# Products of ones on TensorE ahead of long waits, column sums 64 wide, and a two-part split by VectorE alone

## The chip, the cores and the metric

The kernel runs on one core of one Trainium2 chip. The metric is the device time of one execution in microseconds, as the median of several runs. A profiled execution has a time of its own; its span runs from the first to the last instruction that the profile shows.

## What is computed

Three blocks of a transformer follow each other on one sequence of 512 tokens with 1024 features, all in float32. The first mixes an mLSTM (a gated recurrence written as attention with decays) with differential attention, and adds a feed-forward part and a gated side input. The second has four layers; those that matter here are a stick-breaking attention and one with latent queries and keys. The third has a gated feed-forward part, a mixer of spatial gating and forgetting attention, and another feed-forward part. Each part begins with a norm over the features, and this is what the change is about.

```python
def rmsnorm(x, g):
    xf = x.astype(jnp.float32)
    y = xf * lax.rsqrt(jnp.mean(xf * xf, -1, keepdims=True) + EPS)
    return (y * g.astype(jnp.float32)).astype(x.dtype)
...
def first_block(x, p, ...):
    h = rmsnorm(x, norm_mix_g[l])
    proj = h @ w_in[l]
    mq, mk, mv, mo, mi, mf, dq, dk, dv, gates = jnp.split(proj, split_idx, axis=-1)
    ...
    hm = mlstm_chunkwise(heads(mq_c, M_HEADS), heads(mk_c, M_HEADS), heads(mv, M_HEADS), i_pre, f_pre)
    ya = (jax.nn.sigmoid(mo) * hm) @ w_br_m[l]
    ...
    x = x + mixed @ w_out[l]
    h = rmsnorm(x, norm_ffn_g[l])
    u = causal_dwconv(h @ w_up[l], ffn_conv_w[l], ffn_conv_b[l])
    x = x + (jax.nn.gelu(gt) * val) @ w_down[l]
    hg = rmsnorm(x, norm_ple_g[l])
    x = x + jax.nn.sigmoid(hg @ w_ple_gate[l]) * (p[l].astype(x.dtype) @ w_ple[l])
    return rmsnorm(x, norm_final_g)
...
def reference(x, p, ...):
    x = first_block(x, p, ...)
    x = second_block(x, ...)
    return third_block(x, c_3, ...)
```

## The kernel before

**Tiles.** Activations lie with features on the 128 partitions and the 512 tokens along the free axis, as eight tiles of 128x512. A weight matrix is read in pieces of 128x1024 by DMA into `raw`. For precision each operand is split into two parts of a shorter float type, a high part and the rest: `hi` and `lo` for activations (`split`), `wh` and `wl` for weights (`load`). ScalarE (ACT) rounds the high part, VectorE (DVE) subtracts it for the rest. A matmul into a PSUM tile `pm` is then three products, hi x wh, lo x wh, hi x wl (`mm`, L429 to L431; `mm_tok`, L439 to L441, with tokens as the output's rows and 256 columns).

**A norm.** `Norm.add` squares each tile (ACT) and adds it up in `acc` (DVE). `colsum` then sums over the partitions on TensorE (PE): for each block of 128 tokens one product of `acc` with a column of ones, into one PSUM tile; `add_pe` does the same from each squared tile, where the sums of eight tiles are collected in PSUM. `rstd` goes on with `ms_eps` (DVE, tile `ms`, L577) and `rpow` (GpSimd, tile `rc`, L572, the power of -1/2), and `bcast_ps` (L584, tile `bc`) puts the result on all partitions by four products, or two where a turn treats half of the tokens (`rows`). Everything that is scaled by the norm waits for that. What PE has to do meanwhile is other work that doesn't need the norm: the first products of the next projection, whose rows are scaled later.

**Order.** Each engine takes its instructions in the order in which the program has them. A scheduler sets that order from the code, the priorities and its own table of costs, so that a new instruction also moves others. PSUM is shared out in pools: three tiles for `pm`, one for sums and broadcasts (`ms`), two for scores, one each for two other roles. A reader of a PSUM tile waits for the writes into that tile that stand ahead of it in the program.

**The first stage.** `decays` builds, for each of four blocks of tokens, the row `R` of the recurrence's decay: a running sum on DVE, and `parts`, which clears R (L407), rounds the high part on ACT (L408) and subtracts on DVE (L409). `columns` then transposes the columns `cc` on PE into `cps` (L676) and copies them to `ccol` (DVE, L677). ACT needs `ccol` for the decay matrix `DT` (L834), which starts from `pd` (PE, L831); `num` (L838) is the product with the values `vt` (copied from `pm` by ACT, L816). In the same stretch DVE works through a product for the third block (`adaw`, L1408), one weight tile at a time, as its DMA comes in; SyncE issues it when a `raw` tile is free, which is when a `wl` has been made.

Of the kernel before, what the change touches and what calls it, by code (L numbers as in the profile page):

```python
# [23 lines left out]
EPS = 1e-6  # L24
NEG = -1e30
# [212 lines left out]
class Norm:  # L238
# [21 lines left out]
    def add_pe(self, k, x, sl):  # L260

        net, nc = self.net, self.net.nc
        sq = net.q(F32, "sq")
        nc.scalar.activation(sq[:, sl], x[:, sl], AF.Square)
        if k == 0:
            self.cols = net.psa("colsum")
        for j, o in enumerate(range(sl.start, sl.stop, P)):
            nc.tensor.matmul(self.cols[:, j:j + 1], sq[:, o:o + P], net.ones[:, 0:1], start=k == 0 and j == 0, stop=k == 7, skip_group_check=True)

    def rstd(self, sl=ALL):  # L270
        net = self.net
        n = (sl.stop - sl.start) // P
        ps = net.colsum(self.acc, sl) if self.cols is None else self.cols[:, :n]
        self.cols = None
        return net.rpow(net.ms_eps(ps, self.n, n), n)

    def stats(self):
        rc = self.rstd()
        return self.net.bcast([rc[:, j:j + 1] for j in range(NB)]), rc

    def rows(self, sl, role):

        rc = self.rstd(sl)
        return self.net.bcast_ps([rc[:, j:j + 1] for j in range((sl.stop - sl.start) // P)], role)


class Net:
    def __init__(self, ctx, tc, d):
# [14 lines left out]
        self.dp = pool("dp", 1, space=bass.MemoryType.DRAM)  # L303
        self.vec = self.const([P, NV], F32, "vec")
# [84 lines left out]

    def split(self, src):  # L390
        nc = self.nc
        h, l = self.t(F32R, "hi"), self.t(F32R, "lo")
        nc.scalar.copy(h, src)  # L393
        nc.vector.tensor_tensor(l, src, h.bitcast(F32), ALU.subtract)  # L394
        return h, l
# [8 lines left out]
    def parts(self, out, src, n, sl=ALL):  # L404

        nc = self.nc
        nc.vector.memset(out.bitcast(F32)[:, sl], 0.0)  # L407
        nc.scalar.copy(out[0:n, sl], src[0:n, sl])  # L408
        nc.vector.tensor_tensor(out[64:64 + n, sl], src[0:n, sl], out[0:n, sl].bitcast(F32), ALU.subtract)  # L409
# [144 lines left out]
    def colsum(self, acc, sl=ALL):  # L554

        ps = self.psa("colsum")
        n = (sl.stop - sl.start) // P
        for j in range(n):
            o = sl.start + j * P
            self.nc.tensor.matmul(ps[:, j:j + 1], acc[:, o:o + P], self.ones[:, 0:1], start=True, stop=True)  # L560
        return ps[:, 0:n]
# [18 lines left out]
    def bcast_ps(self, cols, role="ms", ps=None):  # L580

        ps = self.psa("bc", role) if ps is None else ps
        for j, col in enumerate(cols):
            self.nc.tensor.matmul(ps[:, j * P:(j + 1) * P], col.to_broadcast([P, P]), self.ident, start=True, stop=True)  # L584
# [35 lines left out]
    def block1(self, third):  # L620
# [10 lines left out]
        with self.tc.issue_after(self.last.ins):  # L631
            self.constants()
            self.wide = True
            self.lead(first, xg, w, [ALL])
# [37 lines left out]
        def columns():  # L672
            ps = self.psa("cps")
            with self.tc.issue_after(self.pe.ins):
# [277 lines left out]
    def ffn1(self, norm):  # L952
# [3 lines left out]
        rb, _ = norm.stats()  # L956
# [32 lines left out]
    def ple(self, norm):  # L989
# [12 lines left out]
        rb, _ = norm.stats()  # L1002
# [17 lines left out]
    def final_norm(self, na, nb):  # L1020
# [4 lines left out]
        pb = self.colsum(nb.acc)  # L1025
        mb = self.s(NB, "mb")
# [42 lines left out]
    def stick_breaking(self, xg, rb, rc, norm):  # L1069
# [43 lines left out]
        for grp in range(4):  # L1113
# [6 lines left out]
            for c in range(2):  # L1120
                last = self.sb_pair(*cur, c, o[2 * grp + c], pre)
            self.fill_all()
            cur = nxt
        with self.tc.issue_after(last.ins):
# [3 lines left out]
    def sb_pair(self, q, k, vt, c, out, pre):  # L1128
# [15 lines left out]
        for tiles, blocks in (((0, 1, 2), (1, 2, 3)), ((3, 4), (0,))):  # L1144
# [38 lines left out]
            for sb in blocks:  # L1183
                for par in range(2):
                    col = (sb % 2) * 256 + (2 * c + par) * 64
                    nc.tensor.matmul(po[ROWS[par], sb * P:], vt[sb // 2][:, col:col + 64], reg(pr, sb, par), start=sb == 1, stop=sb == 0, skip_group_check=True)
# [3 lines left out]
    def mla(self, norm, third):  # L1190
# [6 lines left out]
        rb, rc = norm.stats()  # L1197
# [130 lines left out]
        for f in (work[0], gates[1], work[1], gates[2], work[2]):  # L1328
            f()
        for c in range(4):  # L1330
# [189 lines left out]
    def hybrid(self, x, first):  # L1520
# [93 lines left out]
        def branch_rstd(norm):  # L1614
            norm.rc = norm.rstd()

        def branch(name, norm, ys, at):

            rb = self.bcast([norm.rc[:, j:j + 1] for j in range(NB)])
            for k in range(4):  # L1620
# [40 lines left out]
        branch_rstd(nb)  # L1661
# [155 lines left out]
```

## Time and profile before

| what | us |
|---|---|
| three runs, median (lowest to highest) | 2471.32 (2469.2 to 2471.55) |
| the profiled execution | 2467.3 |
| its span | 2465.5 |
| PE busy | 2401.9 |
| DVE, ACT, GpSimd busy | 1327.3, 990.7, 67.0 |
| start to start of products into `pm`, full clock: 512 columns | 0.23 |
| the same, 256 columns | 0.12 |

The profile has a page of sums (busy time by engine, costliest groups of instructions, DMA issues) and views of the trace: waits by line, a timeline, and the busy time of an engine in chosen stretches with the clock that TensorE was granted there (1.00 is 2.4 GHz, 0.50 is 1.2 GHz). In a timeline row stand the start, the duration, the engine, the line and operation with output and input, how many were joined in the row, and in brackets how long the engine had been idle and what released it. A product in float32 of 128 columns appears as two passes, so x8 is four products.

### The profile page before, as it was taken

The numbers are of one execution on the slowest core, as the hardware profiler recorded it, in microseconds if no ns is written. First come the engines' busy times: TensorE is split into PE (matmuls) and PEld (weight loads), VectorE is DVE, ScalarE is ACT, GpSimd is POOL, SyncE is SP. The second block draws the span as 40 slices with busy tenths as digits, with TensorE's granted clock in tenths as the row PEclk, the third lists the DMA queues.
The fourth block names the chain that finished last, engine by engine and source line by source line (L and its number), as shares of the span: only waits on it lengthen the run. The fifth ranks groups of instructions, "written<-read, shape, count | busy, mean of one in ns | idle before, by whom it ended". The sixth has DMA issues, their size and how long they took to land. (4 is left out here: it accounts for less than half of the span.)

```text
span 2465.5 us, 30961 instructions
## 1 busy us (share of the span) xinstructions
PE 2401.9 (97%) x12430; PEld 1979.6 (80%) x12430; DVE 1327.3 (54%) x2240; ACT 990.7 (40%) x1579; POOL 67.0 (3%) x66
## 2 busy tenths in 40 slices
PE   8999999999999999999999999999999989999998
PEld 6877778888888787776877798888898768888887
DVE  7536556774775664445666954323364565432333
ACT  5423433442343445665334633232235444322221
POOL 0000000000000000000010000000010002000001
PEclk9999999999999999999999999999999999999999
DMA  5222225433433432222301323232222211223221
GB/s 190 95 91 94 94 97 181 141 127 97 161 125 114 132 109 84 71 78 77 107 29 62 114 84 120 86 107 98 87 68 87 81 43 52 94 88 109 94 94 43
DMA packets 71743, 240.74 MB, mean 98 GB/s; under 512 B 8232, under 2 KB 11184, under 8 KB 71600
## 3 DMA queue, kind: packets, MB, share of 16 engines
q1 hardware_dynamic: 71600, 238.78, 29.2%
q8 instruction: 97, 1.59, 0.3%
q14 instruction: 46, 0.38, 0.1%
HBM read 236.64 MB, written 2.11 MB: 97 GB/s over the span
## 5 line engine op out<-in xcount | busy, mean ns | idle before, releaser
L429 PE MATMUL pm<-hi,wh 128*128 128x512 f32 (+1 forms) x2736 | 1044.2, 383 | 9.4 <-ACT hi L393 5.7
L430 PE MATMUL pm<-lo,wh 128*128 128x512 f32 (+1 forms) x2736 | 1041.6, 381 | 0.4 <-DVE lo L394 0.4
L431 PE MATMUL pm<-hi,wl 128*128 128x512 f32 (+1 forms) x2736 | 1040.6, 381 | 0.0
L419 ACT CAST wh<-raw 128x1024 fp32r<-128x1024 f32 (+1 forms) x372 | 382.0, 1029 | 783.9 <-PE pm L430 536.2
L420 DVE TENSOR_TENSOR wl<-raw,wh 128x1024 fp32r<-128x1024 f32 (+1 forms) x372 | 444.8, 1196 | 441.7 <-ACT wh L419 416.8
L429 PEld LDWEIGHTS pm<-hi,wh 128*128 128x128 f32 x2736 | 517.6, 189 | 108.7 <-issue 7.7
L430 PEld LDWEIGHTS pm<-lo,wh 128*128 128x128 f32 x2736 | 517.2, 189 | 97.9 <-issue 3.5
L431 PEld LDWEIGHTS pm<-hi,wl 128*128 128x128 f32 x2736 | 517.1, 189 | 96.5 <-issue 3.4
L439 PE MATMUL pm<-wh,hi 128*128 128x256 f32 x400 | 116.0, 290 | 6.2 <-ACT vt L816 4.9
L1408 DVE CUSTOM_DVE_ANT_0 adaw<-adaw,cb 128x1024 f32<-128x1024 f32 x72 | 87.9, 1220 | 53.9 <-DMA adaw<-in_w_ada 53.6
L441 PE MATMUL pm<-wh,lo 128*128 128x256 f32 x400 | 114.5, 286 | 0.0
L440 PE MATMUL pm<-wl,hi 128*128 128x256 f32 x400 | 114.0, 285 | 0.0
L572 POOL TENSOR_TENSOR rc<-ms,nhalf 128x4 f32<-128x4 f32 (+3 forms) x33 | 42.2, 1278 | 2301.2 <-DVE ms L577 1865.0
L1487 DVE TENSOR_TENSOR sg<-sg,pm 128x512 f32<-128x512 f32 x44 | 30.2, 687 | 133.3 <-PE pm L431 133.3
L439 PEld LDWEIGHTS pm<-wh,hi 128*128 128x128 f32 x400 | 77.6, 194 | 7.2 <-ACT vt L816 5.3
L440 PEld LDWEIGHTS pm<-wl,hi 128*128 128x128 f32 x400 | 77.6, 194 | 0.4 <-issue 0.2
L441 PEld LDWEIGHTS pm<-wh,lo 128*128 128x128 f32 x400 | 77.6, 194 | 0.2
L481 PE MATMUL pm<-hi,wh 128*128 128x256 f32 (+1 forms) x216 | 61.5, 309 | 10.2 <-ACT hi L400 7.1
L970 DVE SCALAR_TENSOR_TENSOR uy<-ur,vec,uy 128x511 f32<-128x511 f32 x88 | 65.7, 748 | 9.0 <-ACT uy L968 8.0
L258 DVE TENSOR_TENSOR acc<-acc,sq 128x512 f32<-128x512 f32 (+1 forms) x93 | 54.8, 595 | 27.6 <-ACT sq L254 26.4
L482 PE MATMUL pm<-lo,wh 128*128 128x256 f32 (+1 forms) x216 | 66.2, 308 | 0.3 <-DVE lo L1439 0.3
L483 PE MATMUL pm<-hi,wl 128*128 128x256 f32 (+1 forms) x216 | 66.1, 309 | 0.0
(350 smaller groups left out, 2344.5 us busy)
## 6 DMA issues: line engine op xcount, KB each, us to landing
raw<-in_w_gu SPq DMA_DIRECT2D x88, 512.0 KB, 3.2
adaw<-in_w_ada SPq DMA_DIRECT2D x72, 512.0 KB, 3.2
raw<-in_w_dn SPq DMA_DIRECT2D x48, 512.0 KB, 3.2
raw<-in_w_up SPq DMA_DIRECT2D x44, 512.0 KB, 3.3
raw<-in_w_g SPq DMA_DIRECT2D x16, 512.0 KB, 3.3
raw<-in_w_l0qk SPq DMA_DIRECT2D x16, 512.0 KB, 3.3
raw<-in_w_l SPq DMA_DIRECT2D x12, 512.0 KB, 3.2
X<-in_x SPq DMA_DIRECT2D x16, 256.0 KB, 6.6
```

The source lines that it names most:

```text
L419: nc.scalar.copy(wh[:, :n], raw[:, :n])
L420: nc.vector.tensor_tensor(wl[:, :n], raw[:, :n], wh[:, :n].bitcast(F32), ALU.subtract)
L429: self.nc.tensor.matmul(out, a, xh, start=start and k == 0, stop=False)
L430: self.nc.tensor.matmul(out, a, xl, start=False, stop=False)
L431: self.pe = self.nc.tensor.matmul(out, b, xh, start=False, stop=stop and k == n - 1)
L439: self.nc.tensor.matmul(out, xh[:, sl], a, start=start and k == 0, stop=False)
L440: self.nc.tensor.matmul(out, xh[:, sl], b, start=False, stop=False)
L441: self.pe = self.nc.tensor.matmul(out, xl[:, sl], a, start=False, stop=stop and k == len(x) - 1)
L482: self.nc.tensor.matmul(o[:, sl], wh[:, k], xl[:, sl], start=False, stop=False)
L483: self.nc.tensor.matmul(o[:, sl], wl[:, k], xh[:, sl], start=False, stop=k == 7)
L970: nc.vector.scalar_tensor_tensor(y[:, sh:], raw[:, :S - sh], self.v("fconv_w", 44 * (2 - sh) + f), y[:, sh:], mult, add)
L1408: nc.vector.tensor_tensor_reduce(w, w, cb, 0.5, 0.0, ALU.mult, ALU.add, mod[:, i:i + 1])
```

## The change

Four edits. **Sums**: the products that sum over partitions take 64 columns of ones instead of one and write 64 equal columns; the reader takes every 64th. **Products of ones**: a new `busy(n)` issues n products of a 128x128 tile of ones with itself into columns 256 to 383 of a PSUM tile that nothing else uses there. It is called at 17 places, for 212 products in all: 36 before the first projection, 24 ahead of the transposes in `columns`, 6, 16, 8, 9, 10 and 16 after the sums of six norms, 26 at the end of the stick-breaking attention, 22 before the first scores of the latent attention, 15 after the broadcast in the mixer's second branch, and 4 after the sums of the second half in six turns. **Split**: `parts` rounds on DVE instead of ACT (four times in `decays`, once in the mixer). **Constant**: the tile of ones is set at the start by DVE.

```diff
 EPS = 1e-6
+CW = 64
 NEG = -1e30
...
         for j, o in enumerate(range(sl.start, sl.stop, P)):
-            nc.tensor.matmul(self.cols[:, j:j + 1], sq[:, o:o + P], net.ones[:, 0:1], start=k == 0 and j == 0, stop=k == 7, skip_group_check=True)
-    def rstd(self, sl=ALL):
+            net.pe2 = nc.tensor.matmul(self.cols[:, j * CW:(j + 1) * CW], sq[:, o:o + P], net.ones[:, :CW], start=k == 0 and j == 0, stop=k == 7, skip_group_check=True)
+    def rstd(self, sl=ALL, busy=0):
         net = self.net
         n = (sl.stop - sl.start) // P
-        ps = net.colsum(self.acc, sl) if self.cols is None else self.cols[:, :n]
+        if self.cols is None:
+            ps, bank = net.colsum(self.acc, sl), net.sums_bank
+        else:
+            ps, bank = self.cols[:, 0:n * CW:CW], self.cols
         self.cols = None
+        net.busy(busy, [net.pe2], bank)
         return net.rpow(net.ms_eps(ps, self.n, n), n)
-    def stats(self):
-        rc = self.rstd()
+    def stats(self, busy=0):
+        rc = self.rstd(busy=busy)
         return self.net.bcast([rc[:, j:j + 1] for j in range(NB)]), rc
...
-        rc = self.rstd(sl)
+        rc = self.rstd(sl, 4 if sl.start else 0)
         return self.net.bcast_ps([rc[:, j:j + 1] for j in range((sl.stop - sl.start) // P)], role)
...
         self.dp = pool("dp", 1, space=bass.MemoryType.DRAM)
+        self.one_sq = self.const([P, P], F32, "one_sq")
+        nc.vector.memset(self.one_sq, 1.0)
         self.vec = self.const([P, NV], F32, "vec")
...
+    def busy(self, n, after=(), bank=None):
+        if n == 0:
+            return
+        bank = self.psa("busy", "tr") if bank is None else bank
+        with ExitStack() as ctx:
+            for i in after:
+                ctx.enter_context(self.tc.issue_after(i.ins))
+            for _ in range(n):
+                self.nc.tensor.matmul(bank[:, 256:256 + P], self.one_sq, self.one_sq, start=True, stop=True, skip_group_check=True)
...
         nc.vector.memset(out.bitcast(F32)[:, sl], 0.0)
-        nc.scalar.copy(out[0:n, sl], src[0:n, sl])
+        nc.vector.tensor_copy(out[0:n, sl], src[0:n, sl])
         nc.vector.tensor_tensor(out[64:64 + n, sl], src[0:n, sl], out[0:n, sl].bitcast(F32), ALU.subtract)
...
-        ps = self.psa("colsum")
+        ps = self.sums_bank = self.psa("colsum")
         n = (sl.stop - sl.start) // P
...
             o = sl.start + j * P
-            self.nc.tensor.matmul(ps[:, j:j + 1], acc[:, o:o + P], self.ones[:, 0:1], start=True, stop=True)
-        return ps[:, 0:n]
+            self.pe2 = self.nc.tensor.matmul(ps[:, j * CW:(j + 1) * CW], acc[:, o:o + P], self.ones[:, :CW], start=True, stop=True)
+        return ps[:, 0:n * CW:CW]
...
         for j, col in enumerate(cols):
-            self.nc.tensor.matmul(ps[:, j * P:(j + 1) * P], col.to_broadcast([P, P]), self.ident, start=True, stop=True)
+            self.pe2 = self.nc.tensor.matmul(ps[:, j * P:(j + 1) * P], col.to_broadcast([P, P]), self.ident, start=True, stop=True)
         return ps
...
             self.wide = True
+            self.busy(36, (), self.psa("busy"))
             self.lead(first, xg, w, [ALL])
...
             ps = self.psa("cps")
+            self.busy(24, [self.pe], ps)
             with self.tc.issue_after(self.pe.ins):
...
         xg = norm.x
-        rb, _ = norm.stats()
+        rb, _ = norm.stats(6)
         nxt = Norm(self, lambda k: self.v("norm_ple", k))
...
                 pe.append(e)
-        rb, _ = norm.stats()
+        rb, _ = norm.stats(16)
         gg = self.const([P, 8], F32, "gg")
...
         pb = self.colsum(nb.acc)
+        self.busy(8, [self.pe2], self.sums_bank)
         mb = self.s(NB, "mb")
...
                 last = self.sb_pair(*cur, c, o[2 * grp + c], pre)
+            ends = [self.pe2]
             self.fill_all()
             cur = nxt
+        self.busy(26, [*ends, self.pe])
         with self.tc.issue_after(last.ins):
...
                     col = (sb % 2) * 256 + (2 * c + par) * 64
-                    nc.tensor.matmul(po[ROWS[par], sb * P:], vt[sb // 2][:, col:col + 64], reg(pr, sb, par), start=sb == 1, stop=sb == 0, skip_group_check=True)
+                    self.pe2 = nc.tensor.matmul(po[ROWS[par], sb * P:], vt[sb // 2][:, col:col + 64], reg(pr, sb, par), start=sb == 1, stop=sb == 0, skip_group_check=True)
         nc.vector.tensor_copy(out, po)
...
         nc.sync.dma_start(sin, d["cs_tab"][:, S:2 * S])
-        rb, rc = norm.stats()
+        rb, rc = norm.stats(9)
         lat = {}
...
             f()
+        self.busy(22, [self.pe2, self.pe])
         for c in range(4):
...
-        def branch_rstd(norm):
-            norm.rc = norm.rstd()
+        def branch_rstd(norm, busy=10):
+            norm.rc = norm.rstd(busy=busy)
...
             rb = self.bcast([norm.rc[:, j:j + 1] for j in range(NB)])
+            if at:
+                self.busy(15, [self.pe2])
             for k in range(4):
...
         self.flush()
-        branch_rstd(nb)
+        branch_rstd(nb, 16)
         self.fill_all()
```

The new instructions move others. On DVE in the first stage, behind the last part of R; `wl` belongs to weights that come in, `adaw` to the third block. Before:

```order
L409 TENSOR_TENSOR R<-G,R 4x128
L420 TENSOR_TENSOR wl<-raw,wh 128x1024
L677 COPY ccol<-cps 128x16
L420 TENSOR_TENSOR wl<-raw,wh 128x1024
L837 SCALAR_TENSOR_TENSOR DT<-sT,DT 128x512
L837 SCALAR_TENSOR_TENSOR DT<-sT,DT 128x384
L1408 ISA adaw,mod<-adaw,cb 128x1024
```

and now:

```order
L427 CAST R<-G 4x128
L428 TENSOR_TENSOR R<-G,R 4x128
L439 TENSOR_TENSOR wl<-raw,wh 128x1024 x2
L1433 ISA adaw,mod<-adaw,cb 128x1024
L1433 ISA mod 128x1
L698 COPY ccol<-cps 128x16
L858 SCALAR_TENSOR_TENSOR DT<-sT,DT 128x512
L858 SCALAR_TENSOR_TENSOR DT<-sT,DT 128x384
```

`ccol` stood behind one `wl` and stands now behind two and the step on `adaw`.

On PE at the same place, from the transposes on; before:

```order
L676 MATMUL cps<-cst,cc 128x4 x4
L831 MATMUL pd<-R,pick 128x512
L832 LDWEIGHTS bf_ident
L832 MATMUL pd<-bf_mask_t,bf_ident 128x128
L836 MATMUL sT<-cy 128x512
L439 MATMUL pm<-wh,hi 128x256
L440 MATMUL pm<-wl,hi 128x256
```

and now:

```order
L407 MATMUL cps<-one_sq 128x128 x24
L697 MATMUL cps<-cst,cc 128x4 x4
L852 MATMUL pd<-R,pick 128x512
L853 LDWEIGHTS bf_ident
L853 MATMUL pd<-bf_mask_t,bf_ident 128x128
L857 MATMUL sT<-cy 128x512
L852 MATMUL pd<-R,pick 128x384
```

Eleven products into `pm` that stood between `sT` and the second `pd` have moved behind it.

On PE at the norm at 821 us (the one ahead of the gated side input); before:

```order
L560 MATMUL colsum<-ones,acc 128x1 x4
L429 MATMUL pm<-hi,wh 128x512
L430 MATMUL pm<-lo,wh 128x512
L431 MATMUL pm<-hi,wl 128x512
L429 MATMUL pm<-hi,wh 128x512
L430 MATMUL pm<-lo,wh 128x512
L431 MATMUL pm<-hi,wl 128x512
L429 MATMUL pm<-hi,wh 128x512
L584 MATMUL bc<-cst,rc 128x128 x4
```

and now:

```order
L579 MATMUL colsum<-ones,acc 128x64 x4
L407 MATMUL colsum<-one_sq 128x128 x16
L448 MATMUL pm<-hi,wh 128x512
L449 MATMUL pm<-lo,wh 128x512
L603 MATMUL bc<-cst,rc 128x128 x4
L450 MATMUL pm<-hi,wl 128x512
```

The sixteen products stand between the sums and `bc`, in the tile of the sums, and five of seven products into `pm` have moved behind `bc`.

## Rows read from the trace of the kernel before

**Rows 1.** the page's first part: engine, busy us (share of the span), instructions
```profile
PE 2401.9 (97%) x12430; PEld 1979.6 (80%) x12430; DVE 1327.3 (54%) x2240; ACT 990.7 (40%) x1579; POOL 67.0 (3%) x66
```

**Rows 2.** PE's waits: waiter, releaser, us in total, times, longest us
```profile
PE bc L584 <- POOL rc L572: 14.0, 17, 2.3
PE pm L481 <- ACT hi L400: 7.1, 1, 7.1
PE pm L429 <- ACT hi L393: 5.7, 2, 3.4
...
PE mls L1340 <- ACT p L1349: 4.6, 3, 2.8
...
PE pm L439 <- ACT p L1349: 1.3, 1, 1.3
```

**Rows 3.** half-clock stretches: us, PE busy (instructions), granted clock, DMA share, GB/s
```profile
85.15:91.98 6.83, 4.63 (x21) 0.50 0.19 72
825.84:829.25 3.41, 3.41 (x12) 0.50 0.42 139
1163.76:1167.17 3.41, 3.12 (x7) 0.50 0.00 0
1214.96:1218.37 3.41, 3.41 (x12) 0.50 0.02 5
1293.47:1296.88 3.41, 3.41 (x16) 0.50 0.00 0
1839.60:1843.01 3.41, 3.41 (x15) 0.50 0.78 279
2006.85:2013.68 6.83, 5.92 (x18) 0.50 0.00 0
2030.75:2037.57 6.82, 4.69 (x11) 0.50 0.06 26
2088.77:2095.60 6.83, 6.58 (x32) 0.50 0.23 79
```

**Rows 4.** PE's timeline, 128x128 passes: start us, us, operation, xcount
```profile
1268.36 1.95 PE L584 MATMUL bc<-cst,rc 128*128 128x128 f32 x16
...
2015.82 1.04 PE L1721 MATMUL tr<-cst,fxp 128*128 128x128 f32 x8
2016.61 0.47 PE L429 MATMUL pm<-hi,wh 128*128 128x512 f32 x1
```

**Rows 5.** timeline of the first stage, 85 to 100 us, and adaw's DMA
```profile
85.96 0.62 ACT L408 CAST R<-G 4x512 fp32r<-4x512 f32 x1 [3.44 <-DVE G L668]
...
87.35 0.58 PE L439 MATMUL pm<-wh,hi 128*128 128x256 f32 x1 [4.90 <-ACT vt L816]
...
93.37 0.28 DVE L409 TENSOR_TENSOR R<-G,R 4x128 fp32r<-4x128 f32 x1 [0.36 <-ACT R L408]
...
95.33 0.41 PE L676 MATMUL cps<-cst,cc 4*128 4x4 f32 x4
...
96.22 0.17 DVE L677 COPY ccol<-cps 128x16 f32<-128x16 f32 x1
96.33 0.33 SPq L1407 DMA_DIRECT2D adaw<-in_w_ada  x1
...
100.12 1.02 PE L838 MATMUL num<-DT,vt 128*128 128x512 f32 x2
...
adaw<-in_w_ada SPq DMA_DIRECT2D x72, 512.0 KB, 3.2
```

**Rows 6.** timeline of the norm at 821 us, PE and DVE
```profile
820.14 0.95 PE L560 MATMUL colsum<-ones,acc 128*128 128x1 f32 x8
820.94 0.49 PE L429 MATMUL pm<-hi,wh 128*128 128x512 f32 x1
...
821.69 1.23 DVE L1408 CUSTOM_DVE_ANT_0 adaw<-adaw,cb 128x1024 f32<-128x1024 f32 x1 [4.67 <-DMA adaw<-in_w_ada]
...
822.85 0.16 DVE L577 TENSOR_SCALAR ms<-colsum 128x4 f32<-128x4 f32 x1
```

## The prediction

> **What bounds the kernel now.** I read the busy times first: TensorE (PE) is busy for 2401.9 us of a span of 2465.5 us [rows 1]. So a stage is worth what PE loses in it, and the other engines count only where PE waits for them. The list of PE's waits [rows 2] shows where that is. The largest entry is the broadcast of a norm (bc, L584) that waits for GpSimd's power (L572): 14.0 us in 17 waits. The others that this change touches are single waits: 7.1 us at the start, 5.7 us in two waits for a gated tile's rounding (hi), 4.6 and 1.3 us for p in the second attention of the middle block. The third view is the half-clock stretches [rows 3]: nine of them before the last rows of the output, at a granted clock of 0.50 (1.2 GHz instead of 2.4), with PE busy for 38.59 us of 44.36. Work at half clock would take half the time at the full one, so 38.59 / 2 = 19.3 us is the most that the clock can give back. The change spends products of ones on it; the question is whether they lie in idle time or ahead of it.
>
> **The price of one product.** A product of ones is a float32 matmul of 128x128, in two passes. No such product is in the trace, but its shape is. Eight passes of L1721 took 0.79 us from their start to the next matmul's start (2015.82 to 2016.61), 0.198 us for two; sixteen of L584 took 1.95 us, 0.244 us for two [rows 4]. I take 0.22 us. 212 products are then 46.6 us of PE time, against 19.3 us of clock. Unless more than half of them are covered by waits that stay as they are, the change loses.
>
> **Products on the norm's chain: 89 of them.** The chain is colsum, ms on VectorE (DVE), the power on GpSimd, bc on PE. PE works in order, and in the built program ms waits for the last of the products, not for the last sum, because both lie in one PSUM tile. So the products don't fill the wait: they stand ahead of it, and the wait comes after them as long as before. That holds for 6, 16, 8, 9, 10 and 16 products at six norms and 4 at each of six turns: 89 x 0.22 = 19.6 us. Two sites are cheaper. At the second of them (16 products, at 821 us) ms is late already: it starts at 822.85, behind a DVE step on adaw that began at 821.69, while PE had left the sums at 820.94 [rows 6]. Its 16 products end at 820.94 + 3.52 = 824.46, so ms moves by 1.6 instead of 3.5; but of seven products of pm that stood beneath the wait five have moved behind it, at 0.23 us each (the table) 1.1 us. That makes 2.7 instead of 3.5. At the third (8) three more pm stand beneath the wait, about 0.7 us, and I take 0.9 instead of 1.8. Sum: 19.6 - 0.8 - 0.9 = **17.9 us**. The bounds: at 0.198 and 0.244 for a product 16 and 20; the lower end falls to 0 only if ms doesn't wait, which is a rival below.
>
> **Products for which only PE waits: 36, 26, 22 and 15.** The 36 at the start lie against a wait of 7.1 us [rows 2], which begins with the span; at 0.22 they take 7.9 us, at half clock 15.8. I take 0, with -0.5 and +2 as bounds, from these two. The 26 (5.7 us) stand ahead of the longer wait for hi, 3.4 us [rows 2]; the tile is then ready and its followers are paced by DVE, so I take +1.4, between 0 and 2.3. The 22 (4.8 us) stand ahead of the first scores of that second attention, where PE had no wait; 1.3 us of a later wait for p goes under them, and some 1.2 us of score products have moved behind, beneath the 2.8 us wait [rows 2]: +2.2, between 1 and 4.8. The 15 (3.3 us) stand against the second wait for hi, 5.7 - 3.4 = 2.3 us: +1.0. Sum: **+4.6 us**.
>
> **The first stage, 82 to 105 us: 24 products, and R by DVE alone.** Here two things pull apart. PE's wait of 4.90 us ended at 87.35 when ACT had copied vt, and vt stood behind ACT's copy of R at 85.96 [rows 5]. ACT had sat idle for 3.44 us ahead of that copy, so with it on DVE vt starts at 82.5 and PE resumes at about 83.4. The 48 products of pm with 256 columns up to the transposes (cps) then take 48 x 0.12 (the table) = 5.8 us at full clock, to 89.2; 24 x 0.22 = 5.3 brings cps to 94.5, against 95.33 before: 0.9 us won, with no room left for the half clock of [rows 3] there. But DVE's order is changed too: ccol, which ran at 96.22, now stands behind two wl and the adaw step. That adaw's load was issued at 96.33, when the first wl had ended [rows 5]; loads of adaw land 3.2 us after issue [rows 5] and the step takes 1.23 us [rows 6]. DVE has the last part of R at about 93.65 in either kernel (four more casts, each no dearer than the 0.28 us of the last subtraction per 128 columns [rows 5], against DVE's waits for ACT, which go), so wl ends at 95.1, adaw's data are there at about 98.5, the step ends at 99.7 and ccol at 99.9: 3.7 us later than before. The decay's exponent on ACT and the scores' row pd wait for ccol. I find num, which began at 100.12 [rows 5], at 101.7, with 11 pm (1.3 us) and a pair of sT (0.75 us) that were done by then and now follow: +3.7 us. PE is idle for 4.7 us ahead of it, as long as the wait that drew the first stretch of [rows 3]; another such stretch costs 4.63 / 2 = 2.3 us. I count half of that: **+4.8 us**. Bounds: -0.9, if adaw is there in time, and +6.0.
>
> **Sums with 64 columns, the cast in the hybrid, one memset.** Eight passes of one column took 0.80 us from the first's start to the next matmul's (820.14 to 820.94, [rows 6]), eight of 128 columns 0.79 [rows 4]; 64 lie between, so 0 within 0.5 us over all sums. The fifth cast (cs) moves between two engines on one chain: 0 within 0.5.
>
> **What the clock gives back.** Without the first stretch, which is in the stage above, [rows 3] holds 33.96 us of work at half clock, so 17.0 us at most. Ahead of seven of the eight stretches the products make PE busy in the idle time or just before it. The one at 2006.85 I leave: both waits ahead of it stay as they are, the norm's and the next one, for DVE's fxp. 17.0 - 5.92 / 2 = **14.0 us** back; the bounds are 0 and 17.0. The Trainium skill ("TensorE: Matmul & The Clock Gate", section "Terms") puts the loss at the throttled time times one less the clock's share. By it the eight stretches hold (44.36 - 6.83) / 2 = 18.8 us and the sum would be lower by 1.8 us than the largest return by rows; the trace doesn't agree there, as PE was idle for 5.77 of the 44.36 us, and idle time gains nothing from a clock.
>
> **The sum.** 17.9 + 4.6 + 4.8 - 14.0 = +13.3 us on the profiled execution of 2467.3 us, 2480.6. That execution lies 4 us under the median of the runs shown, 2471.32, so the forecast for the median is 2471.3 + 13.3 = **2484.6 us**, 0.5% slower. About 0.2% (5 us) is what a measurement of this kernel can tell from no change.
>
> **The rivals.** First, on the other side: **the norm's products lie inside the wait**. If ms could start with the sums, the 17.9 us would vanish beneath 14.0 us of waits that are there anyway, and a warmer PE would give back all 17.0: 4.6 + 4.8 - 17.0 = -7.6, 2463.7 us. For it: the products write columns 256 to 383 and ms reads columns below 256. Against it: the wait in the built program, and the order of PE. It decides from the point where more than 15 of the 17.9 us are covered. Second, **no stall at ccol**: adaw's data come earlier or DVE has slack; the stage gives -0.9 instead of +4.8 and the total is +7.6, 2478.9. For it speaks that a landing time isn't in the order; against it that the load is issued behind wl as before. Third, **the clock does not come back**: the waits stay after the products, and where PE then idles 1 to 2 us the stretches fall as before, at other places. Then +27.3, 2498.6 us. For it: the waits are as long as they were; against it: the 17 waits of the first row of [rows 2] average 0.8 us, and most are not followed by a stretch.
>
> **How the numbers follow.** Forecast 0.45, products inside the wait 0.26, no stall 0.18, no clock 0.11. The forecast's own terms spread by about 7 us either way, the others by 5. Slower by over 0.2%: nearly all of the first (0.43), the last (0.11) and two thirds of the stall case (0.12), 0.65 or so. Faster: three quarters of the second, 0.20. The rest, 0.15, is within 0.2%. The range must reach into the second case and almost to the last: 2463 to 2497 leaves out about 0.12 below and 0.07 above.
>
> **What would show it.** In the profile of the changed kernel, ms (now L596) should start some 0.05 us after the last product at each norm, not after the sums, and bc's waits for the power should still come to 12 us or more. ccol should start near 99.9 with PE idle before pd, and no idle of 4.9 us at 82. The half-clock list should hold two to four stretches instead of nine. The prediction falls if bc starts no later after its sums than before, if ccol comes before adaw's data, or if a product takes 0.11 us.

## The result, and the profile after

The changed kernel took **2487.69 us** (median of four runs, 2487.33 to 2489.66) beside 2470.26 for the kernel before (median of four, 2468.21 to 2471.55): a ratio of 1.0078, with a 95% interval of 1.0066 to 1.009. The forecast was 2484.6 us, slower. The profiled execution took 2487.8 us with a span of 2486.1, against 2465.5 before: +20.6 in the spans. Of the experiments' runs one, of ten without the norm's products, came at 3831.69 us with a mean granted clock of 0.582 and is left out of that kernel's median.

The page's first part of the changed kernel, to be held against [rows 1]:

```profile
PE 2436.7 (98%) x12854; PEld 2017.0 (81%) x12854; DVE 1329.8 (53%) x2246; ACT 988.3 (40%) x1574; POOL 66.7 (3%) x66
```

PE is busy for 34.8 us more and has 424 more instructions, two for each of the 212 products. Span less PE busy is 63.6 us before and 49.4 now. So 14.2 us of idle time went, and more than twice that came as work.

PE's waits in the changed kernel (waiter, releaser, us in total, times, longest), the answer to [rows 2]:

```profile
PE bc L603 <- POOL rc L591: 13.3, 16, 1.4
...
PE pd L852 <- ACT DT L855: 4.1, 1, 4.1
...
PE tr L1748 <- DVE fxp L1778: 1.8, 1, 1.8
```

The two entries for hi (7.1 and 5.7 us) are gone. The norms' wait is nearly as long as before, 13.3 us for 14.0, and there is a new one: pd waits 4.1 us.

The half-clock stretches ahead of the last rows of the output, with the columns of [rows 3], given one after another:

```profile
2026.07:2032.89 6.82, 5.85 (x18) 0.50 0.01 2
1305.85:1309.27 3.42, 3.24 (x11) 0.50 0.00 0
100.95:104.36 3.41, 3.41 (x10) 0.50 0.35 138
```

Three are left of nine, with PE busy for 12.50 us in 13.65.

Which instructions waited for the products of ones (L407), from the view of that line in the changed kernel:

```profile
L407 PE MATMUL colsum<-one_sq x178: 275/275/328, 458.2 to 2475.3; 128*128 128x128 f32 x178
...
who waited for it (us, times):
  DVE ms L596: 18.7, 10
```

The 89 products in the tile of the sums are 178 passes, and what waits for them is ms, the next link of the norm's chain.

### The profile page after: what moved, and what is told of

It is laid out like the page before. It is cut to its first block, busy times and chain, and to the rows that moved or that the text cites. A ratio compares the mean times of both kernels' runs of the same rounds, so it can differ in the third digit from the quotient of the medians.

```text
span 2486.1 us, 31814 instructions
## 1 busy us (share of the span) xinstructions
PE 2436.7 (98%) x12854; PEld 2017.0 (81%) x12854; DVE 1329.8 (53%) x2246; ACT 988.3 (40%) x1574; POOL 66.7 (3%) x66
```

## The experiments

A span is PE busy plus the rest, "idle" below. Of the busy time, the products take 0.22 us each (measured in the first group of experiments); what is left of the difference in busy time is clock, since otherwise the same products run. The table is worked out in this way from the page's first part of each kernel, against before (span 2465.5, busy 2401.9, idle 63.6). Ratios and intervals are those of the medians, against the kernel before on the same chip.

| kernel | ratio [95%] | span | products, us | clock, us | idle, us |
|---|---|---|---|---|---|
| changed | 1.0078 [1.0066, 1.009] | 2486.1 | 212: +46.6 | -11.8 | -14.2 |
| no chain products | 1.0028 [1.0017, 1.0039] | 2470.4 | 123: +27.1 | -9.6 | -12.6 |
| own tile | 1.0045 [1.003, 1.006] | 2478.2 | 212: +46.6 | -12.4 | -21.5 |
| doubled on the chain | 1.0158 [1.0141, 1.0176] | 2504.1 | 301: +66.2 | -13.6 | -14.0 |
| without the 24 | 1.0038 [1.0028, 1.0049] | 2476.3 | 188: +41.4 | -12.8 | -17.8 |
| without the 99 | 1.0087 [1.0074, 1.0101] | 2487.0 | 113: +24.9 | -4.6 | +1.2 |
| no products | 1.0022 [1.0012, 1.0031] | 2469.6 | 0 | +1.9 | +2.2 |
| 64 columns only | 1.0018 [1.0009, 1.0027] | 2472.1 | 0 | +3.3 | +3.3 |
| split only | 0.9998 [0.9989, 1.0007] | 2464.1 | 0 | +0.8 | -2.2 |
| changed, one column | 1.0089 [1.0075, 1.0103] | 2489.6 | 212: +46.6 | -6.3 | -16.2 |
| fitted | 0.9991 [0.9982, 1.0001] | 2463.9 | 89: +19.6 | -6.5 | -14.7 |
| fitted, 10 in `columns` | 0.9989 [0.9979, 0.9999] | 2464.1 | 93: +20.5 | -7.9 | -14.0 |
| fitted, one column | 0.9981 [0.997, 0.9992] | 2466.9 | 89: +19.6 | +0.9 | -19.1 |

Each row is one execution, and executions of one kernel differ: those of the kernel before ran from 2465.28 to 2475.87 us, at a mean granted clock of 0.989 to 0.984. So a few us in the clock's column can be the execution's and not the edit's. And 0.005 us more for a product would move the clock of the changed kernel from -11.8 to -12.9.

### The norm's chain: none, doubled, in a tile of its own

The theory: the products stand ahead of the wait because ms waits for the last write into its tile. The rival: they lie inside it. Three edits of the changed kernel, the first without the 89 products:

```diff
-        net.busy(busy, [net.pe2], bank)
...
-        self.busy(8, [self.pe2], self.sums_bank)
```

> The changed kernel (2487.7 us) without the 89 products after the sums of norms; the other 123 stay. Chain theory (ms waits for the last product, 0.22 us each lie on the path): 17.9 us leave, and some 7 us of half clock come back at the norms (1.7 at 826, 1.7 at 1215, 3.3 at 2089): about 2477 us, half-clock stretches again at several norms, bc's waits for the power no shorter. Rival (products lie inside the wait and the time goes to the moved instructions): without them the time stays at 2485 to 2490 or gets worse by the clock.

The second gives them a tile of their own instead of the sums':

```diff
-        net.busy(busy, [net.pe2], bank)
+        net.busy(busy, [net.pe2])
...
-        self.busy(8, [self.pe2], self.sums_bank)
+        self.busy(8, [self.pe2])
```

> The changed kernel with all 212 products, but those after the sums write a PSUM tile of their own (the one of the 36 and 26 uses), so that ms may start with the sums. Chain theory: at each norm the products then fill the wait of 0.5 to 1.4 us that now follows them, 6 to 8 us less in all, about 2480 us; what is longer than the wait still stands ahead of bc; ms starts within 0.1 us of the sums; the total of bc's waits for the power falls from 13.3 to under 5 us. Rival (the wait in the built program costs nothing): no change, 2486 to 2489 us.

The third issues twice as many:

```diff
-        net.busy(busy, [net.pe2], bank)
+        net.busy(2 * busy, [net.pe2], bank)
...
-        self.busy(8, [self.pe2], self.sums_bank)
+        self.busy(16, [self.pe2], self.sums_bank)
```

> The changed kernel with twice as many products after the sums of norms (178 instead of 89). Chain theory: 89 more at 0.22 us on the path, +19.6 us, less a little for pm products that slide beneath: 2503 to 2508 us, with bc's waits for the power still 12 to 14 us. Rival (most lie in idle time): under +8 us, 2488 to 2495.

Measured: 2474.87, 2480.06 and 2507.72 us. One norm, that of the mixer's first branch, shows why. PE's timeline there (start, duration, operation, xcount passes, idle before and releaser), without the products:

```profile
2007.58 1.10 PE L578 MATMUL colsum<-ones,acc 128*128 128x64 f32 x8
2010.12 2.08 PE L602 MATMUL bc<-cst,rc 128*128 128x128 f32 x8 [1.44 <-POOL rc L590]
```

In the changed kernel, with ten of them, and what DVE did:

```profile
2019.29 1.10 PE L579 MATMUL colsum<-ones,acc 128*128 128x64 f32 x8
2020.23 2.45 PE L407 MATMUL colsum<-one_sq 128*128 128x128 f32 x20
2024.12 1.16 PE L603 MATMUL bc<-cst,rc 128*128 128x128 f32 x8 [1.44 <-POOL rc L591]
...
2022.72 0.16 DVE L596 TENSOR_SCALAR ms<-colsum 128x4 f32<-128x4 f32 x1 [4.09 <-PE colsum L407]
```

With twenty:

```profile
2030.08 1.10 PE L579 MATMUL colsum<-ones,acc 128*128 128x64 f32 x8
2031.02 4.68 PE L407 MATMUL colsum<-one_sq 128*128 128x128 f32 x40
2037.14 1.16 PE L603 MATMUL bc<-cst,rc 128*128 128x128 f32 x8 [1.44 <-POOL rc L591]
```

With ten, in a tile of their own (the first two passes of bc; no idle time stands in brackets):

```profile
2015.17 1.07 PE L579 MATMUL colsum<-ones,acc 128*128 128x64 f32 x8
2016.09 2.45 PE L407 MATMUL busy<-one_sq 128*128 128x128 f32 x20
2018.37 0.39 PE L603 MATMUL bc<-cst,rc 128*128 128x128 f32 x2
```

From sums to bc it is 2.54, 4.83 and 7.06 us with none, ten and twenty. The wait for the power is 1.44 us in all three: the products don't shorten it, they delay it. In the changed kernel ms starts at 2022.72, as the last product ends (2020.23 + 2.45 = 2022.68). The step from ten to twenty is 2.23 us, 0.223 for a product. In a tile of their own the same ten cover the wait and bc comes 3.20 after the sums. Over the kernel, doubling cost 20.0 us in the medians for 89 more products, which agrees as far as runs that lie 5 us apart can tell. Taking them away won 12.8 us of 17.4. The own tile won 7.6 us, as its idle time fell by 7.3; what is longer than a wait still stands ahead of bc. PE's waits of bc for the power fell to 6.6 us there, not under 5 as expected. The rival that the products lie inside the wait falls for the kernel as changed.

### The first stage: without the 24, and the split alone

Without the 24 products in `columns` (of the changed kernel):

```diff
             ps = self.psa("cps")
-            self.busy(24, [self.pe], ps)
```

> The changed kernel without the 24 products ahead of the transposes in the first stage, which also puts ccol back ahead of the adaw step on VectorE. Order theory (the stall of 4.1 us at 96 us is ccol behind adaw's load): the stall goes, num starts at 98 to 99 us instead of 102, 6 to 8 us less: about 2480.5 us. Rival (the stage is longer because of the 24 products' own 5.5 us and nothing else): 5.3 us less at most, and the stall for ccol stays at its place.

The split alone: one column, no products, R still rounded by DVE (of the changed kernel; the constant stays):

```diff
-CW = 64
+CW = 1
...
-        if n == 0:
-            return
+        return
```

> The kernel before with the split by VectorE alone: no products, one column. Theory: the wait of 4.9 us at 82 us goes, waits for cc of 2.5 us take its place, ccol 1.4 us earlier: 1 to 4 us under the kernel before, 2464 to 2467 us. Rival (all of it is given back later): within 1 us.

Timeline of the changed kernel's first stage (start, duration, engine, operation), the answer to [rows 5]:

```profile
83.20 0.38 PE L458 MATMUL pm<-wh,hi 128*128 128x256 f32 x1 [0.85 <-ACT vt L837]
...
89.05 5.52 PE L407 MATMUL cps<-one_sq 128*128 128x128 f32 x48
...
93.61 2.36 DVE L439 TENSOR_TENSOR wl<-raw,wh 128x1024 fp32r<-128x1024 f32 x2
94.50 0.41 PE L697 MATMUL cps<-cst,cc 4*128 4x4 f32 x4
94.86 0.33 SPq L1432 DMA_DIRECT2D adaw<-in_w_ada  x1
...
98.30 1.23 DVE L1433 CUSTOM_DVE_ANT_0 adaw<-adaw,cb 128x1024 f32<-128x1024 f32 x1 [2.33 <-DMA adaw<-in_w_ada]
...
99.45 0.17 DVE L698 COPY ccol<-cps 128x16 f32<-128x16 f32 x1
99.71 0.69 ACT L855 ACTIVATE DT<-pd,ccol 128x512 f32<-128x512 f32 x1 [8.69 <-DVE ccol L698]
...
100.45 0.44 PE L852 MATMUL pd<-R,pick 128*128 128x384 f32 x1 [4.13 <-ACT DT L855]
...
102.06 1.91 PE L859 MATMUL num<-DT,vt 128*128 128x512 f32 x2
```

The old wait of 4.90 us is down to 0.85 (at 83.20), and the transposes come at 94.50 instead of 95.33. Then DVE takes up the step on adaw at 98.30, when its data are there, and ccol behind it at 99.45 instead of 96.22; ACT has been idle for 8.69 us by then, PE for 4.13. The power after this stage starts at 206.58 us, before at 201.00: +5.6. (The first norm's power, ahead of the stage, starts at 31.82 and 31.92.)

The kernel without the 24 has ccol ahead of adaw again (rows of its timeline, same columns):

```profile
95.45 0.17 DVE L697 COPY ccol<-cps 128x16 f32<-128x16 f32 x1
95.56 0.33 SPq L1431 DMA_DIRECT2D adaw<-in_w_ada  x1
95.71 0.69 ACT L854 ACTIVATE DT<-pd,ccol 128x512 f32<-128x512 f32 x1 [3.99 <-DVE ccol L697]
```

It took 2477.79 us, 9.9 less than the changed kernel, where 6 to 8 were expected. The stage itself has 5.6 of them (its next power starts at 201.01 us instead of 206.58): PE has 5.3 us of products less and the wait of 4.1 us is gone, but PE waits 2.5 us for cc, works 5.92 us at half clock where the changed kernel worked 3.41, and num starts at 100.09, later than the 98 to 99 expected. The other 4 us come behind the stage, where nothing was edited; 1.6 of them are the stretch at 1305.85 (3.24 / 2), which this kernel doesn't have. So not all of the 9.9 us is shown to be the 24 products' doing. Nor does the run say that each of the 24 is harmful, only that with them the scheduler puts ccol behind a load. The split alone comes out level, 0.9998. Its vt wait falls from 4.9 to 0.8 us, but the transposes then wait for cc, which DVE makes (2.5 us in two waits), and the half-clock stretch stays, 5.3 us later than in [rows 3]:

```profile
90.48:97.31 6.83, 6.40 (x22) 0.50 0.39 107
```

So of the 4.1 us of wait that the split takes away 2.5 come back at another place, and in the time nothing is left that can be told.

### 64 columns: no products, sums alone, and one column in the changed kernel

No products of ones (sums and split stay), from the changed kernel:

```diff
-        if n == 0:
-            return
+        return
```

> The changed kernel without any product of ones: sums with 64 columns and the split by VectorE are left. Theory (the products' place is what the change costs, and 64 columns alone keep the clock up at the norms of 826, 1215 and 1840 us, as in the run without the 89): 1 us less in the first stage and 4 to 5 us of clock, 2463 to 2467 us, against 2468 to 2470 of the kernel before. Rival (the products bought the clock): nine half-clock stretches as before, 2468 to 2470 us.

The same with R rounded by ACT again, so that only the sums are left:

```diff
-        nc.vector.tensor_copy(out[0:n, sl], src[0:n, sl])
+        nc.scalar.copy(out[0:n, sl], src[0:n, sl])
```

> The kernel before with 64 columns in the sums alone: no products, split with ScalarE's copy. Theory that 64 columns keep the clock up at three norms: 4 to 5 us under the kernel before, the wait of 4.9 us at 82 us still there, half-clock stretches missing near 826, 1215 and 1840. Rival: within 1 us of the kernel before, nine stretches.

And the changed kernel with one column:

```diff
-CW = 64
+CW = 1
```

> The changed kernel with one column in the sums, everything else kept: all 212 products at their places and the split by VectorE. Theory (64 columns cost through the order they bring at the two turns near 1820 and 2080 us, some 4 us each in the run with the sums alone): 3 to 6 us under the changed kernel, 2482 to 2485 us; the wait of bc at 1822 (1.31 us) and the wait for ACT's hi near 1846 gone. Rival (64 columns keep the clock up and pay for themselves): 2487 to 2493 us, more half-clock stretches than the changed kernel's three.

Measured: 2472.99, 2472.73 and 2490.48 us. The first was expected to be faster than before and wasn't; the sums alone cost 4.9 us, which neither theory had. The time isn't in the sums' passes: the 280 of them take 0.107 us on average from start to next start before and 0.108 in the changed kernel (those behind which PE idles left out). By the table half of it is idle time. At the second half of the first turn, the kernel with the sums alone (PE's, VectorE's and GpSimd's timelines):

```profile
1819.16 1.00 PE L269 MATMUL colsum<-ones,sq 128*128 128x64 f32 x8
...
1822.12 0.71 PE L602 MATMUL bc<-cst,rc 128*128 128x128 f32 x4 [1.31 <-POOL rc L590]
...
1820.28 1.22 DVE L438 TENSOR_TENSOR wl<-raw,wh 128x1024 fp32r<-128x1024 f32 x1
...
1820.51 1.56 POOL L590 TENSOR_TENSOR rc<-ms,nhalf 128x2 f32<-128x2 f32 x1 [3.36 <-DVE ms L595]
```

and the kernel before:

```profile
1817.66 0.50 PE L268 MATMUL colsum<-ones,sq 128*128 128x1 f32 x4
...
1819.30 0.68 PE L584 MATMUL bc<-cst,rc 128*128 128x128 f32 x4
...
1818.28 0.41 DVE L1500 TENSOR_TENSOR H<-pm,H 128x256 f32<-128x256 f32 x1
...
1818.50 0.71 POOL L572 TENSOR_TENSOR rc<-ms,nhalf 128x2 f32<-128x2 f32 x1 [5.11 <-DVE ms L577]
```

Two things differ: five products of pm stand between the last sums and bc where ten stood, and the power of the same shape takes 1.56 us instead of 0.71. The other kernels agree on the second: 0.71 in the four with one column, 1.56 or 1.57 in the ten with 64. What goes with it is VectorE's order: with 64 columns a step that makes a wl has just begun when the power starts, with one column a short step on H has, and wl starts after the power (1818.61). The last section follows this through all norms.

The other half is clock: PE is busy at half clock for 47.86 us with the sums alone and for 38.59 before. This half isn't shown to be the edit's own: with the products present it turns round, as 64 columns save 5.5 us of clock (-11.8 against -6.3, one execution each) and cost 2.0 of idle, so that taking them out of the changed kernel made it no faster (1.0089 against 1.0078, intervals that overlap). The theory that the columns' cost would come back there fell; the time lies in the range of the rival, by which the columns pay for themselves.

### The 99 products for which only PE waits

The changed kernel without the 36, 26, 22 and 15:

```diff
-            self.busy(36, (), self.psa("busy"))
...
-        self.busy(26, [*ends, self.pe])
...
-        self.busy(22, [self.pe2, self.pe])
...
-            if at:
-                self.busy(15, [self.pe2])
```

> The changed kernel without the 99 products of ones for which only TensorE waits: the 36 at the start, 26 at the end of the stick-breaking attention, 22 before the latent attention's first scores, 15 in the mixer's second branch. The 89 on the norms and the 24 ahead of the transposes stay. By the prediction's steps the time falls by the +4.6 us of these four sites, and the clock gives back less, since the products near 1840 and 2030 to 2090 go: two or three half-clock stretches come back, at about 1.7 us of work at half clock each, 3.4 to 5 us. Theory: the two cancel, 2484 to 2490 us, ratio 1.007 to 1.009. Rival A: these products buy no clock, and the time falls by all of 4.6 us or more, below 2484 us. Rival B: they are worth more than they cost, above 2490 us.

2488.97 us, ratio 1.0087, not to be told from the changed kernel; theory held. Its waits for hi are back:

```profile
PE pm L500 <- ACT hi L419: 6.9, 1, 6.9
PE pm L448 <- ACT hi L412: 5.7, 2, 3.5
```

By the table the 99 cost 21.8 us, cover 15.4 of idle and return 7.2 of clock. At the start the clock shows in the durations (the trace's record of the granted clock begins behind these rows). PE's timeline of this kernel, then of the changed one:

```profile
6.95 0.79 PE L500 MATMUL pm<-hi,wh 128*128 128x512 f32 x1 [6.95 <-ACT hi L419]
...
10.04 0.63 PE L501 MATMUL pm<-lo,wh 128*128 128x512 f32 x1
```

```profile
1.05 10.35 PE L407 MATMUL busy<-one_sq 128*128 128x128 f32 x72 [1.05 <-DVE one_sq L310]
11.16 0.48 PE L500 MATMUL pm<-hi,wh 128*128 128x512 f32 x1
11.47 0.40 PE L501 MATMUL pm<-lo,wh 128*128 128x512 f32 x1
```

The projection starts 4.2 us later but its products run at 0.40 instead of 0.63 us, and the first norm's power starts at 31.82 against 31.48: the 36 cost 0.3 us.

### Products fitted to the waits

The fitted kernel puts the chain's products into a tile of their own and cuts them to what the waits hold, with none at the turns, at the norm that had 8 and ahead of the latent attention's first scores:

```diff
-        net.busy(busy, [net.pe2], bank)
+        net.busy(busy, [net.pe2])
...
-        rc = self.rstd(sl, 4 if sl.start else 0)
+        rc = self.rstd(sl)
...
-            self.busy(24, [self.pe], ps)
+            self.busy(6, [self.pe], ps)
...
-        rb, _ = norm.stats(6)
+        rb, _ = norm.stats(3)
...
-        rb, _ = norm.stats(16)
+        rb, _ = norm.stats(4)
...
-        self.busy(8, [self.pe2], self.sums_bank)
...
-        self.busy(26, [*ends, self.pe])
+        self.busy(14, [*ends, self.pe])
...
-        rb, rc = norm.stats(9)
+        rb, rc = norm.stats(4)
...
-        self.busy(22, [self.pe2, self.pe])
...
-        def branch_rstd(norm, busy=10):
+        def branch_rstd(norm, busy=6):
...
-                self.busy(15, [self.pe2])
+                self.busy(10, [self.pe2])
...
-        branch_rstd(nb, 16)
+        branch_rstd(nb, 6)
```

> The changed kernel with products only where a wait is, in a tile of their own, and about as many as the wait has room for: 6 in the first stage instead of 24, 3, 4 and 4 at three norms (6, 16 and 9 before), 6 and 6 at the mixer's two norms (10 and 16), 14 instead of 26 and 10 instead of 15, none at the others, 36 at the start. Chain theory: these cost nothing on the path, ccol is back ahead of the adaw step, and two or three stretches of half clock more than without products stay away: 2458 to 2463 us, faster than both kernels. Rival (a product costs what it lasts wherever it stands): 59 products beside the 36 at 0.22 us, 13 us above the run without products.

It took 2466.01 us. With 10 products instead of 6 in `columns`:

```diff
-            self.busy(6, [self.pe], ps)
+            self.busy(10, [self.pe], ps)
```

> As e7_fitted, with 10 products in the first stage instead of 6; by the built order ccol then stands behind two wl instead of one. Order theory: ccol one wl (1.2 us) later, 0.5 to 1.5 us more than e7_fitted, unless the four products keep the clock up there (3 us less). Rival (only the number of products counts): 0.9 us more.

That took 2465.50 us. Its ccol stands behind two wl and comes 1.06 us later than in the fitted kernel (95.82 for 94.76), as expected, but neither this nor the price of four products can be told in the time.

The fitted kernel (6 in `columns`) with one column:

```diff
-CW = 64
+CW = 1
```

> As e7_fitted (products fitted to waits, in their own tile, split by VectorE) with one column in the sums, so that the order at the turns is that of the kernel before. Theory: the 4 to 7 us that the run with the sums alone lost at the turns come off e7_fitted's 2466.0: 2459 to 2462 us, 0.2 to 0.4% faster than the kernel before. Rival (64 columns are what keeps the clock up): 2466 to 2470 us, with half-clock stretches near 826 and 1215 us again.

2464.59 us, ratio 0.9981 [0.997, 0.9992]: 0.19% faster than before, about the size that can be told from no change. It is the lowest ratio, but the three intervals overlap, so that none is shown to be best. The first and the last came out about 3 us above the top of what was expected, for two reasons. The first was worked out from the kernel without products, for which 2463 to 2467 had been expected and 2472.99 came; against that kernel it is 7.0 us faster. The last missed on the clock: its idle time is 4.4 us less than the fitted kernel's, as the theory wanted, but its clock column gives up 7.4. That column is the worst case, since its execution (2468.97 us) lies 4.4 above the median. In all, 89 fitted products cost 19.6 us and cover 15 to 19 of idle, which leaves the clock to decide.

## Why the prediction was right, and where it was off

**The mechanism held.** The rows that it named came as it said: ms 0.04 us after the last product (0.05), bc's waits 13.3 us (12 or more), ccol at 99.45 (99.9), no idle of 4.9 us at 82, three half-clock stretches (two to four).

**The price of a product.** 0.22 us, between the two shapes of [rows 4]; measured 0.223 from ten to twenty at one norm, and 0.222 at the norm of [rows 6], where 16 of them hold PE from 827.86 to 831.41.

**The norm's chain: 17.9 us forecast, 18.0 measured** (19.6 of products less 1.6 of idle, from the kernel without them to the changed one, one execution each). The medians differ by less, 12.8, since these products also bring 2.2 us of clock by the table and the kernel without them was profiled in its fastest run. At the norm of [rows 6] 2.7 was forecast, worked out from pm products that went behind bc; the answer to those rows in the changed kernel:

```profile
827.03 1.00 PE L579 MATMUL colsum<-ones,acc 128*128 128x64 f32 x8
827.86 3.79 PE L407 MATMUL colsum<-one_sq 128*128 128x128 f32 x32
...
831.69 0.16 DVE L596 TENSOR_SCALAR ms<-colsum 128x4 f32<-128x4 f32 x1 [0.81 <-PE colsum L407]
...
832.00 1.01 POOL L591 TENSOR_TENSOR rc<-ms,nhalf 128x4 f32<-128x4 f32 x1 [371.00 <-DVE ms L596]
```

From sums to ms it is 4.66 us for 2.71 before, +1.95, against the 1.6 forecast for that part. But bc comes only 1.12 us later behind its sums (6.03 for 4.91), as the power takes 1.01 us for 1.85 before, a term that the prediction didn't have. With the five pm products behind bc, 1.15 us, the norm costs 2.3 us for the 2.7 forecast.

**The four sites for which only PE waits: +4.6 forecast, +6.4 measured** without clock (21.8 of products less 15.4 of idle). Mis-sized by 1.8, all of it at the start: the 36 take 7.9 us at full clock but cover 5.9, as PE's first wait falls from 6.95 to 1.05 and not to nothing, the rest being the wait for the tile of ones. That they run at the low rate at first (10.1 us to the next matmul) stands in the clock's column, and the faster products behind them give most of it back, as shown above.

**The first stage: +4.8 forecast, +5.6 measured.** The steps held within half a microsecond: PE back at 83.20 (83.4), transposes at 94.50 (94.5), adaw's step at 98.30 (98.5), num at 102.06 (101.7), PE idle 4.13 (4.7). A new half-clock stretch, counted by half, did come, of 3.41 us. In the kernel without the 24, where ccol stands ahead of the step on adaw, the wait of 4.13 us is gone.

**Sums with 64 columns: 0 within 0.5 forecast. This step failed** as a bound. It priced the passes alone, and those are indeed alike; the sums alone cost 4.9 us in the median, by the order at the turns, a longer power, and clock that may be the execution's. In the changed kernel the idle part of that is 2.0 us.

**The clock: 14.0 us forecast beside the first stage, about 15 with it; 11.8 measured.** PE is busy at half clock for 26.09 us less than in [rows 3], which by halves is 13.0. The measured 11.8 lies 1.2 below this, and for the kernel without the 99 it is 4.6 measured and 5.7 by busy time. The page of the Trainium skill that the prediction weighed ("TensorE: Matmul & The Clock Gate", section "Terms") would give (44.36 - 13.65) / 2 = 15.4 here and (44.36 - 30.73) / 2 = 6.8 there, both further off. What the forecast missed is two stretches: the one at 1305.85, which it took to be gone, and the new one in the first stage, which it counted by half.

So the two errors on the costs (1.8, and about 2 for the columns) and the one on the clock (about 3) have one sign. They are most of the 7.3 us between the +13.3 forecast and the +20.6 of the spans; in the medians the difference is +17.4, 3.1 us above the forecast time. That the time came so close is in part luck: the forecast carried the 4 us between the kernel before's profiled execution and its median over to the changed kernel, whose profiled execution lies at its median (2487.84 and 2487.69). The rival on the other side fell at its own condition: ms does wait for the products. No stall at ccol fell with the rows above, and the clock that doesn't come back with three stretches for nine.

**What stays open.** Which waits draw a half-clock stretch. The pair of waits of 1.44 and 1.77 us at the mixer's first branch went with one in the kernel before (2006.85 in [rows 3]), in the changed kernel (2026.07), without the chain's products (where it began at 2009.96, ahead of the second wait) and with them doubled; in the kernel without the 99, and in the changed kernel with one column, the same pair did not. The rows of the kernel without the 99:

```profile
2024.97 1.16 PE L603 MATMUL bc<-cst,rc 128*128 128x128 f32 x8 [1.44 <-POOL rc L591]
2027.90 1.09 PE L1743 MATMUL tr<-cst,fxp 128*128 128x128 f32 x8 [1.77 <-DVE fxp L1773]
```

There tr took 1.09 us, in the changed kernel 1.97. So the clock can be summed over a kernel, but the share of one edit in it isn't shown.

## What to carry to other kernels

Work that is to fill a wait must not be what the awaited chain itself waits for: put it in a tile that no link of the chain reads, and look in the trace whether the reader's start moves with the last filler or stays. Size it by the wait, since each filler beyond it costs its full time; here 212 products cost 46.6 us to remove 14.2 of idle and to win 11.8 of clock, and even the fitted ones won no more than 0.1 to 0.2%. And where an edit reorders an engine, look for the first instruction that now stands behind a load: one copy of 0.17 us behind an adaw load brought a wait of 4.1 us, as much as had been taken away there.

## What the runs showed that I had not expected

GpSimd's power has two lengths for one shape, and what VectorE does as it starts tells which. At the norm of [rows 6] it took 1.85 us before, with this step of VectorE just ahead:

```profile
822.92 1.21 DVE L420 TENSOR_TENSOR wl<-raw,wh 128x1024 fp32r<-128x1024 f32 x1
...
823.15 1.85 POOL L572 TENSOR_TENSOR rc<-ms,nhalf 128x4 f32<-128x4 f32 x1 [369.03 <-DVE ms L577]
```

In the changed kernel no step of VectorE runs when it starts at 832.00, and it takes 1.01. Idle time ahead of it doesn't sort them (369 us and 371). In the 14 traces together 58 powers of 128x2 or 128x4 start while a wl is being made, and all of them take 1.54 to 1.62 us (128x2) or 1.84 to 1.85 (128x4), ending 0.55 to 0.57 or 0.85 to 0.87 us after that wl; without a wl those of 128x2 take 0.69 to 0.88, those of 128x4 1.01 or, at the first norm, 1.40. So where an edit reorders VectorE, some 0.85 us of a norm's chain can come or go with it. This is read from all traces, but no run moved the wl alone.

The costs of two edits needn't add: 64 columns cost 4.9 us by themselves, and taking them out of the changed kernel won nothing.
